# One of the seven products per tile of gate and up done in plain float32

## The chip, the cores and the metric

The kernel runs on one core of one Trainium2 chip. The core has four engines that compute, each with its own stream of instructions: TensorE (PE in the profile; its weight loads are PEld), VectorE (DVE), ScalarE (ACT) and GpSimd (POOL). A fifth, SyncE (SP), issues the DMAs here. The metric is the device time of one execution in microseconds (us); lower is better.

## The reference

Two layers of a decoder trunk on 512 tokens of width 1024. Each layer has two feed-forward blocks ("macaron half-steps"), a token mixer of three head groups, and a gated input embedding. The change lies in the feed-forward blocks, of which there are four in all. Their hidden width is 2816:

```python
def swiglu(x, w_in, w_out):
    gate, up = jnp.split(x @ w_in, 2, axis=-1)
    return (jax.nn.silu(gate) * up) @ w_out

  x += 1/2 * post(SwiGLU_a(pre(x)))
  ...
  x += 1/2 * post(SwiGLU_b(pre(x)))
```

`pre` and `post` are RMS norms with a gain. All inputs are float32.

## The kernel before

**Products in parts.** Most products on TensorE take operands of type `fp32r`. Each operand is split into a high and a low part: ScalarE copies the source into the high part, which rounds it (`split`, L140), and VectorE, or POOL where the caller says so, subtracts that from the source to get the low part (L141). `mm3` (L162 to L164) then makes three matmuls for each block of 128 rows: high by high, high by low, low by high. The product of the two low parts is left out.

**Tiles of the hidden features.** `ffn` goes over 22 tiles (m = 0 to 21) of 128 gate features and the same 128 up features. The weights of a tile come in two DMAs (L311), as g1, g2, u1, u2: gate and up by halves of the 1024 inputs, each 128x512. The 512 tokens are halved too, L and H. The four blocks of the product are made by Winograd's form of Strassen's method, with seven products of half size in place of eight. POOL makes four sums of the tile's weights (L353 to L356, `ws`). The seven left operands are g1, g2, u2 as they are (products 1, 2, 4) and the sums s1 to s4 (products 5, 6, 7, 3). Each is split into parts (`wsplit`), so a tile has seven splits, called w1 to w7 after their products. Their buffers come from a pool of six. A product has four blocks of 128 inputs, three matmuls each with 256 tokens: 12 matmuls, 84 for a tile.

**The right operands.** They are made once per block by `turn`, from the normed and transposed input, for tokens by quarters. Halves of the inputs by halves of the tokens serve products 1, 2, 3 and 5 (`xh`, `xl`); three sums, t2, t3 and t4, serve products 6, 7 and 4, and are split into the three tiles `tx`. t4 is written over a part of `xr` (L237) and then split, ScalarE's copy and POOL's subtraction, in the loop at the end of `turn`.

**The combination.** VectorE adds the products out of PSUM: L362 (product 6), L367 (product 2), L365 (products 7 and 5), L369 (product 3), L370, L373 (product 4); ScalarE applies silu (L371); VectorE multiplies gate by up into `h` (L376). Product 3 writes the other half of the bank that L362 reads, and starts only after L362. The four PSUM tiles are `p12` (products 1 and 2), `p63`, `p75` and `p4`.

**The order.** The code is written tile by tile, but a scheduler with a timeline of its own sets the order of each engine's instructions when the program is built. In the middle of the loop it works one tile ahead: VectorE splits the weights of tile m + 1 while it combines tile m. On TensorE the order is 6, 7, 5, the beginning of 4, 3, the rest of 4, and then 1 and 2 of the next tile. The raw weights `wr` go through slots that are also used by the `tx` tiles (six of tag `q`): three are left for the weights, so a slot serves the tile three later.

After the 22 tiles, `ffn_out` makes the second product from `h` with the output weights, again with splits on ScalarE and VectorE, sums on POOL, and matmuls at L466. Its first splits and sums are mixed into the last tiles of the loop.

**Plain float32 elsewhere.** The mixer has some matmuls on float32 operands that are not split, among them L970 in `rwkv_back`: two calls of 256 columns for each half of the tokens.

Of the kernel before, what the change touches and what calls it, by code (L numbers as in the profile page):

```python
# [10 lines left out]
F32R = mybir.dt.float32r  # L11
I32 = mybir.dt.int32
AF = mybir.ActivationFunctionType
ALU = mybir.AluOpType
# [7 lines left out]
EPS = 1e-6  # L22
# [51 lines left out]
class Trunk:  # L74
# [50 lines left out]
    def lanes(self, main=MAINL, aux=AUXL, chain=""):  # L125
        """The PSUM tags that the two kinds of tiles go through in turn."""
        self.main, self.aux = cycle(main), cycle(aux)
        self.chain = chain
# [19 lines left out]
    def wblock(self, ap, name, slot=False, raw=None, eng=None):  # L148
        """A block of weights as two halves, each with its high and low parts."""
        c = ap.shape[1]  # L150
        if raw is None:
            raw = self.wraw.tile([128, c], F32, tag="raw", name=name + "_r")
        self.nc.sync.dma_start(out=raw, in_=ap)
        if slot:
            w = self.slot("h", [2, c], name, F32R)
            self.split(w[:, 0], w[:, 1], raw, eng)
            return [(w[:, 0, i * c // 2:(i + 1) * c // 2], w[:, 1, i * c // 2:(i + 1) * c // 2]) for i in range(2)]
        return [self.wsplit(raw[:, i * c // 2:(i + 1) * c // 2], name, eng) for i in range(2)]
# [17 lines left out]
    def rms(self, ss, scale=1.0):  # L176
        """scale / sqrt(mean + EPS) from two halves of the mean square, each over scale squared."""
        g_ = self.nc.gpsimd
        v, r = self.small("v"), self.small("r")
        g_.tensor_scalar(v, ss[0], ss[1], EPS / (scale * scale), op0=ALU.add, op1=ALU.add)  # L180
        g_.tensor_tensor(r, v, self.mhalf, ALU.pow)
        return r

    def ssq(self, src, name, scale=1.0, dve=False):
        """A half's part of the mean square, over scale squared."""
        junk = self.tmp.tile([128, 512], F32, tag="sg", name="junk")
        s = self.small(name)
        if dve:
            self.nc.vector.tensor_tensor_reduce(junk, src, src, 1.0 / (D * scale * scale), 0.0, ALU.mult, ALU.add, s)
            return s  # L190
        self.nc.scalar.activation(junk, src, AF.Square, scale=D ** -0.5 / scale, accum_out=s)
        return s
# [12 lines left out]
    def turn(self, t, xn, ffn):  # L205
        nc = self.nc
        v_, a_, g_ = nc.vector, nc.scalar, nc.gpsimd
        ps = []
        for j in range(2):
            p = self.aux_tile("xtp").rearrange("p (a b) -> p a b", a=4)  # L210
            for i in range(4):
                k = 4 * j + i
                nc.tensor.transpose(p[:, i], xn[:, k * 128:(k + 1) * 128], self.ident)  # L213
            ps.append(p)
        kss = [slice(0, 4), slice(4, 8)]
        ts = slice(t * 128, (t + 1) * 128)
        if ffn and t == 0:
            self.xr = self.slot("h", [2, 8, 128], "xr")
        if ffn and t == 2:
            self.tx = [self.slot("q", [2, 4, 256], "tx", F32R) for _ in range(3)]  # L220
        if not ffn or t < 2:
            for p, ks in zip(ps, kss):
                self.split(self.xh[:, ks, ts], self.xl[:, ks, ts], p)
                if ffn:
                    a_.activation(self.xr[:, t, ks], p, AF.Copy)
            return
        EB, E1, E3, E4 = None, g_, g_, g_
        # the sums of Winograd's form of the product by blocks
        u = t - 2
        xr = self.xr  # L230
        t2, t3 = (self.tmp.tile([128, 4, 128], F32, tag="tb0", name="tx", bufs=4) for _ in range(2))
        t1, t4 = (xr[:, u, ks] for ks in kss)
        a_.activation(t3, ps[0], AF.Copy)
        v_.tensor_tensor(t1, ps[0], t1, ALU.subtract)
        v_.tensor_tensor(t2, ps[1], t1, ALU.subtract)
        v_.tensor_tensor(t3, ps[1], t3, ALU.subtract)
        g_.tensor_tensor(t4, t4, t2, ALU.subtract)  # L237
        self.split(self.xh[:, kss[1], ts], self.xl[:, kss[1], ts], ps[1], EB)
        us = slice(u * 128, u * 128 + 128)
        self.split(self.xh[:, kss[0], ts], self.xl[:, kss[0], ts], t1, E1)  # L240
        for q, x, e in zip(self.tx, (t2, t3, t4), (None, E3, E4)):
            self.split(q[:, 0, :, us], q[:, 1, :, us], x, e)
# [14 lines left out]
    def out_proj(self, nb, part, blocks, gain, scale, after, tail):  # L257
        """Token-major product of the feature-major parts with weight blocks, post norm, residual."""
# [60 lines left out]
    def ffn(self, l, w, after):  # L319
        """The first product goes by Winograd's form of Strassen's seven products: gate and up features by halves of  # L320
        the inputs, halves of the inputs by halves of the tokens."""
        nc, tc = self.nc, self.tc
        v_, a_, g_ = nc.vector, nc.scalar, nc.gpsimd
# [6 lines left out]
        right = {1: plain(k1, L), 2: plain(k2, L), 3: plain(k2, H), 4: tx[2], 5: plain(k1, H), 6: tx[0], 7: tx[1]}  # L330
        hs = []

# [16 lines left out]
        def unit(m, r, pa, a):  # L349
# [9 lines left out]
            # an even tile has the tokens' second half first  # L359
# [12 lines left out]
            product(4, u2, pd[:, L])  # L372
# [24 lines left out]
    def ffn_out(self, hs, blocks, gain, scale, after):  # L397
        """Token-major product of the features with the output weights, by halves of the model's columns. Some of the
        pairs of feature tiles go by Winograd's form of Strassen's products: halves of the tokens by the tiles of the
        pair by halves of the columns."""  # L400
# [5 lines left out]
        # where the halves of a pair's tiles lie, so that the three that products take as they are lie together  # L406
# [149 lines left out]
    def fm_proj(self, ap, name, halves=False):  # L556
        """Feature-major projection of one 128-column tile."""
        w = self.wblock(ap, name)
        ps = self.mm_tile(name)
        for sl in ((slice(0, 256), slice(256, 512)) if halves else (slice(0, 512),)):  # L560
            for k in range(8):
                self.mm3(ps[:, sl], [q[:, k % 4 * 128:k % 4 * 128 + 128] for q in w[k // 4]],
                         [q[:, k, sl] for q in (self.xh, self.xl)], k == 0, k == 7)
        return ps

    def tm_proj(self, aps, cols, name, eng=None):
        """Token-major projection; aps hold the rows in k order. Tokens share a bank where they fit."""
# [83 lines left out]
    def weave(self, l):  # L651
        """The chains of the three mixers, their pieces in the order of the plan; a chain that writes its output over
        the projections' inputs lets the last projection go first."""
# [47 lines left out]
    def rwkv_prep(self, l):  # L701
        """RWKV-7 heads in chunks of 64 tokens. A unit is a chunk c of a pair p of heads; its removal-key and key
        rows are stacked on the partitions, the removal-key rows on half (c + p) % 2."""
# [22 lines left out]
        for p in range(2):  # L726
# [9 lines left out]
            # decay and in-context rate  # L736
# [9 lines left out]
            # normalised removal key  # L746
# [18 lines left out]
            # k (1 + (a - 1) k_a)  # L765
# [6 lines left out]
            # bonus  # L772
# [8 lines left out]
    def rwkv_scores(self):  # L781
# [5 lines left out]
        # token-major keys and values; the values are centered over each head, which centers the outputs  # L787
# [18 lines left out]
        # masked scores of [keys, queries] and the part of the solve's right side that values give  # L806
# [33 lines left out]
        # the removal queries token-major  # L840
# [11 lines left out]
    def rwkv_solve(self, q):  # L852
        """The merged inverse for four chunks, applied to the values' part and to the removal queries, which it
        replaces. Yields between tiles."""
# [6 lines left out]
        # a half of a bank's partitions belongs to one half of the rows  # L861
# [17 lines left out]
    def rwkv_scan(self):  # L879
        """The recurrence over the chunks."""  # L880
# [15 lines left out]
        for c in range(8):  # L896
            st, ns = sts[c % 2], sts[(c + 1) % 2]
            tk = slice(c * 64, (c + 1) * 64)
            if c < 7:
                # the diagonal blocks of the pairs' states  # L900
                pS = self.aux_tile("pst")[:, 0:128].rearrange("p (a t) -> p a t", a=2)
# [44 lines left out]
    def rwkv_norm(self, yt, eng):  # L946
        """Group norm of the centered heads."""
# [13 lines left out]
    def rwkv_back(self, yt, j):  # L961
        """The way back to feature-major, bonus and output gate."""
# [15 lines left out]
    def invert_blocks(self, sm, z, w):  # L978
        """The blocks of 16 of z = (I - M^T)^-1, for the strictly triangular blocks of 64 whose M^T are in sm."""
# [22 lines left out]
    def invert_merge(self, q, sm, z, w):  # L1002
        """Blocks of 16 merged into blocks of 64, for eight units."""
# [31 lines left out]
    def mlstm_proj(self, l):  # L1035
# [4 lines left out]
        # queries and keys through the causal convolution  # L1040
# [27 lines left out]
        # values, gates  # L1068
# [19 lines left out]
        # running maximum  # L1088
# [38 lines left out]
    def mlstm(self, l):  # L1127
        """The chunks of mLSTM, 128 tokens each."""
# [161 lines left out]
    def attention(self, l):  # L1290
# [10 lines left out]
        # high and low parts: the queries' on the halves of the partitions, the keys' on both  # L1301
# [26 lines left out]
        def softmax(t, g):  # L1328
            # the keys of this tile and the last one, the even tile's first
# [188 lines left out]
```

## Time and profile before

| | |
|---|---|
| runs | 2371.49, 2371.92, 2373.13 us; median 2371.92 |
| the profiled execution | span 2369.3 us from the first instruction to the last, 2.6 us below the median of the runs |
| mean granted TensorE clock | 0.977 of full speed |
| TensorE busy | 2142.1 us (90%), 16592 matmul records |
| VectorE busy | 2019.5 us (85%) |
| ScalarE busy | 1159.0 us (49%) |
| POOL busy | 1215.5 us (51%) |
| HBM | 199.23 MB read, 87 GB/s over the span |

The page is read from its shares down to single instructions. A row of a group has the line, the engine, the operation, what is written and read (out<-in, by the program's names without numbers), the shape, the count, and behind the first bar the busy time in us and the mean ns of one; behind the second stands the idle time of the engine just before such instructions, and what ended it. A row of a timeline has the start in us, the length in us, and the instruction; an entry in square brackets is the idle time before it and its releaser. The length of a matmul includes its way through the array, so matmuls overlap, and the time that each one costs is the distance between starts. The same holds, by some 0.08 us, for VectorE. A row of windows has the stretch, its length, the busy time and the count of PE, PEld, DVE, ACT and POOL, the granted clock, the share of the DMA engines and GB/s. A row for one line has min/median/max in ns, the first and last start, and the form.

The four blocks' loops end, by the `h` of their last tile, near 301, 1003, 1471 and 2171 us.

### The profile page before, as it was taken

How to read it: one execution, taken by the hardware profiler on the slowest of the kernel's cores; microseconds unless marked ns; L12 is line 12 of the kernel's file. 1: busy time of each engine (PE TensorE's matmuls, PEld its weight loads, DVE VectorE, ACT ScalarE, POOL GpSimd, SP SyncE). 2: the span in 40 equal slices, each digit the busy share in tenths (PEclk: the TensorE clock that was granted, in tenths of full speed). 3: DMA queues.
4: the chain of work that ended last, by engine and by line, in shares of the span. 5: the costliest groups of instructions: out<-in, count | busy, mean ns of one | idle time of the engine just before them, and what ended most of it. 6: DMA issues, size and time to landing. Idle time of an engine off the chain costs nothing. (4 is left out here: it accounts for less than half of the span.)

```text
span 2369.3 us, 42540 instructions
## 1 busy us (share of the span) xinstructions
PE 2142.1 (90%) x16592; PEld 1975.2 (83%) x16592; DVE 2019.5 (85%) x2990; ACT 1159.0 (49%) x2262; POOL 1215.5 (51%) x1088
## 2 busy tenths in 40 slices
PE   5899988999998899988989989889999989989898
PEld 5888887988778888887878888888887789889787
DVE  8999999645768999998689999986557699999984
ACT  4444544546545444545554445444474454445443
POOL 5665476132236665566365655751332466555751
PEclk8999999999999999999999999999999999999999
DMA  3222222422031222123411221233220312222232
GB/s 151 90 89 90 71 90 90 147 81 55 20 142 54 86 93 90 63 90 116 134 71 72 92 105 55 84 120 122 68 63 7 143 72 90 90 90 75 78 107 80
DMA packets 67513, 208.78 MB, mean 88 GB/s; under 512 B 15728, under 2 KB 16752, under 8 KB 67312
## 3 DMA queue, kind: packets, MB, share of 16 engines
q1 hardware_dynamic: 67312, 206.07, 25.2%
q8 instruction: 130, 2.13, 0.4%
q14 instruction: 71, 0.58, 0.1%
HBM read 199.23 MB, written 6.82 MB: 87 GB/s over the span
## 5 line engine op out<-in xcount | busy, mean ns | idle before, releaser
L162 PE MATMUL p<-xh,w 128*128 128x256 f32 x1408 | 407.8, 291 | 79.8 <-DVE gate L362 77.5
L164 PE MATMUL p<-xh,w 128*128 128x256 f32 x1408 | 401.6, 286 | 13.6 <-DVE w L141 13.6
L163 PE MATMUL p<-xl,w 128*128 128x256 f32 x1408 | 400.8, 285 | 0.1
L141 DVE TENSOR_TENSOR w<-wr,w 128x512 fp32r<-128x512 f32 x249 | 374.8, 1528 | 10.0 <-ACT w L140 9.8
L140 ACT ACTIVATE w<-ws 128x512 fp32r<-128x512 f32 x352 | 210.6, 623 | 305.0 <-POOL ws L354 178.2
L162 PEld LDWEIGHTS p<-xh,w 128*128 128x128 f32 x1408 | 269.9, 192 | 95.5 <-DVE gate L362 89.7
L141 DVE TENSOR_TENSOR w<-ws,w 128x512 fp32r<-128x512 f32 x352 | 327.7, 935 | 3.2 <-ACT w L140 3.1
L162 PE MATMUL p<-tx,w 128*128 128x256 f32 x1056 | 299.9, 285 | 19.1 <-ACT tx L140 14.7
L164 PE MATMUL p<-tx,w 128*128 128x256 f32 x1056 | 298.9, 284 | 5.3 <-DVE w L141 5.2
L163 PE MATMUL p<-tx,w 128*128 128x256 f32 x1056 | 299.2, 284 | 4.7 <-DVE tx L141 4.7
L164 PEld LDWEIGHTS p<-xh,w 128*128 128x128 f32 x1408 | 270.9, 192 | 14.8 <-DVE w L141 14.8
L353 POOL TENSOR_TENSOR ws<-wr 128x512 f32<-128x512 f32 x88 | 119.0, 1352 | 316.2 <-issue 299.5
L163 PEld LDWEIGHTS p<-xl,w 128*128 128x128 f32 x1408 | 270.8, 192 | 0.7 <-DVE xl L141 0.7
L162 PEld LDWEIGHTS p<-tx,w 128*128 128x128 f32 x1056 | 204.7, 194 | 21.2 <-ACT tx L140 15.3
L164 PEld LDWEIGHTS p<-tx,w 128*128 128x128 f32 x1056 | 203.3, 193 | 7.4 <-DVE w L141 7.1
L163 PEld LDWEIGHTS p<-tx,w 128*128 128x128 f32 x1056 | 203.7, 193 | 5.6 <-DVE tx L141 5.6
L466 PE MATMUL y<-wo,hq 128*128 128x256 f32 x1536 | 189.4, 282 | 3.2 <-DVE up L373 2.7
L140 ACT ACTIVATE w<-wr 128x512 fp32r<-128x512 f32 x264 | 163.3, 625 | 57.7 <-PE p L164 41.9
L466 PEld LDWEIGHTS y<-wo,hq 128*128 128x128 f32 x1536 | 184.5, 189 | 4.8 <-DVE up L373 3.5
L355 POOL TENSOR_TENSOR ws<-wr 128x512 f32<-128x512 f32 x88 | 145.9, 1658 | 46.7 <-DVE w L141 45.0
L354 POOL TENSOR_TENSOR ws<-ws,wr 128x512 f32<-128x512 f32 x88 | 147.4, 1675 | 0.6
L356 POOL TENSOR_TENSOR ws<-wr,ws 128x512 f32<-128x512 f32 x88 | 142.4, 1618 | 5.6
(436 smaller groups left out, 5613.4 us busy)
## 6 DMA issues: line engine op xcount, KB each, us to landing
wr<-in_w_ffn_in SPq DMA_DIRECT2D x176, 512.0 KB, 4.1
ws_r<-in_w_ffn_out SPq DMA_DIRECT2D x56, 512.0 KB, 3.2
wo_r<-in_w_ffn_out SPq DMA_DIRECT2D x32, 512.0 KB, 3.3
pkrv_r<-in_w_rw SPq DMA_DIRECT2D x16, 512.0 KB, 3.5
wpg_r<-in_w_ple_gate SPq DMA_DIRECT2D x16, 512.0 KB, 3.4
xd<-x SPq DMA_DIRECT2D x8, 512.0 KB, 2.9
x<-xd SPq DMA_DIRECT2D x8, 512.0 KB, 3.5
pq_r<-in_w_q SPq DMA_DIRECT2D x8, 512.0 KB, 3.5
```

What stands on the lines that cost most here:

```text
L140: self.nc.scalar.activation(hi, src, AF.Copy)
L141: (eng or self.nc.vector).tensor_tensor(lo, src, hi.bitcast(F32), ALU.subtract)
L162: mm(out, a[0], b[0], start=first, stop=False)
L163: mm(out, a[0], b[1], start=False, stop=False)
L164: mm(out, a[1], b[0], start=False, stop=last)
L353: g_.tensor_tensor(s1, u1, u2, ALU.add)
L354: g_.tensor_tensor(s2, s1, g1, ALU.subtract)
L355: g_.tensor_tensor(s3, g1, u1, ALU.subtract)
L356: g_.tensor_tensor(s4, g2, s2, ALU.subtract)
L466: nc.tensor.matmul(banks[n][:, u], a[:, x, u * 128:u * 128 + 128], b[y], start=n not in seen, stop=last and i == 2, skip_group_check=True)
```

## The change

Product 4, u2 by t4, is done with plain float32 operands. t4 is kept as it is in a float32 tile of its own, `t4`, which takes the slot that the third `tx` tile had; its split (one copy on ScalarE, one subtraction on POOL, for each of two quarters of the tokens) is gone. u2 is read by TensorE from the raw weights; its split w4 (one copy on ScalarE, one subtraction on VectorE) is gone. In place of 12 matmuls on parts there are four calls on float32. The diff, without the lines that only take away comments (lines of code move by up to four):

```diff
-            self.tx = [self.slot("q", [2, 4, 256], "tx", F32R) for _ in range(3)]
+            self.tx = [self.slot("q", [2, 4, 256], "tx", F32R) for _ in range(2)]
+            self.t4 = self.slot("q", [4, 256], "t4")
...
-        g_.tensor_tensor(t4, t4, t2, ALU.subtract)
+        g_.tensor_tensor(self.t4[:, :, u * 128:u * 128 + 128], t4, t2, ALU.subtract)
...
-        for q, x, e in zip(self.tx, (t2, t3, t4), (None, E3, E4)):
+        for q, x, e in zip(self.tx, (t2, t3), (None, E3)):
...
-        right = {1: plain(k1, L), 2: plain(k2, L), 3: plain(k2, H), 4: tx[2], 5: plain(k1, H), 6: tx[0], 7: tx[1]}
+        right = {1: plain(k1, L), 2: plain(k2, L), 3: plain(k2, H), 5: plain(k1, H), 6: tx[0], 7: tx[1]}
...
+        t4 = self.t4
...
-            product(4, u2, pd[:, L])
+            for k in range(4):
+                nc.tensor.matmul(pd[:, L], u2[:, k * 128:(k + 1) * 128], t4[:, k], start=k == 0, stop=k == 3)
```

The scheduler orders the engines anew. VectorE in the middle of a block's loop before the change, from the split w5 of one tile to the split w6 of the next (the numbers in names are those of tiles; gate_1203 belongs to one tile of features, wr_1328 and wr_1458 to the next two):

```order
L141 TENSOR_TENSOR w5_1405<-ws_1364,w5_1405 128x512
L373 TENSOR_TENSOR up_1244<-p4_1243,up_1244 128x256
L141 TENSOR_TENSOR w3_1422<-ws_1365,w3_1422 128x512
L376 TENSOR_TENSOR h_939<-gate_1203,up_1244 128x512
L141 TENSOR_TENSOR w4_1440<-wr_1328,w4_1440 128x512
L141 TENSOR_TENSOR w1_1463<-wr_1458,w1_1463 128x512
L362 TENSOR_TENSOR gate_1332<-p63_1370,gate_1332 128x256
L141 TENSOR_TENSOR w2_1478<-wr_1458,w2_1478 128x512
L367 TENSOR_TENSOR gate_1332<-p12_1331,gate_1332 128x256
L141 TENSOR_TENSOR w6_1504<-ws_1494,w6_1504 128x512
```

And the same stretch of the changed kernel, where L362, L367, L369, L370, L373 and L376 have become L364, L369, L371, L372, L377 and L380:

```order
L141 TENSOR_TENSOR w5_1313<-ws_1272,w5_1313 128x512
L371 TENSOR_TENSOR gate_1122<-p63_1160,up_1163 128x256
L372 TENSOR_TENSOR up_1163<-p75_1161,up_1163 128x256
L141 TENSOR_TENSOR w3_1330<-ws_1273,w3_1330 128x512
L377 TENSOR_TENSOR up_1163<-p4_1162,up_1163 128x256
L380 TENSOR_TENSOR h_880<-gate_1122,up_1163 128x512
L141 TENSOR_TENSOR w1_1360<-wr_1355,w1_1360 128x512
L141 TENSOR_TENSOR w2_1375<-wr_1355,w2_1375 128x512
L364 TENSOR_TENSOR gate_1240<-p63_1278,gate_1240 128x256
L141 TENSOR_TENSOR w6_1401<-ws_1391,w6_1401 128x512
```

The split w4 is gone; w2 now stands ahead of the instruction that product 3 waits for, and the two additions for product 3 (L371, L372) stand behind w5 and no longer ahead of it.

TensorE before, at the end of product 3 and over the rest of product 4 (`tx`) to product 1 of the next tile:

```order
L164 MATMUL p63_1112<-xh_87,w3_1164 128x256
L162 MATMUL p4_1114<-tx_217,w4_1182 128x256
L163 MATMUL p4_1114<-tx_217,w4_1182 128x256
L164 MATMUL p4_1114<-tx_217,w4_1182 128x256
L162 MATMUL p4_1114<-tx_217,w4_1182 128x256
L163 MATMUL p4_1114<-tx_217,w4_1182 128x256
L164 MATMUL p4_1114<-tx_217,w4_1182 128x256
L162 MATMUL p4_1114<-tx_217,w4_1182 128x256
L163 MATMUL p4_1114<-tx_217,w4_1182 128x256
L164 MATMUL p4_1114<-tx_217,w4_1182 128x256
L162 MATMUL p12_1202<-xh_87,w1_1204 128x256
```

And in the changed kernel:

```order
L163 MATMUL p63_1160<-xl_88,w3_1212 128x256
L164 MATMUL p63_1160<-xh_87,w3_1212 128x256
L376 MATMUL p4_1162<-t4_217,wr_1118 128x256 x2
L162 MATMUL p12_1239<-xh_87,w1_1241 128x256
L163 MATMUL p12_1239<-xl_88,w1_1241 128x256
```

Three matmuls of product 4 stood ahead of product 3 and nine behind it; now two calls stand ahead and two behind, and they read the raw weights `wr`. On POOL the order of the four sums of a tile is now s1, s2, s3, s4; it was s1, s3, s2, s4.

## The prediction

> **What bounds the kernel now.** I read the page first, then the stretches by windows, then one tile's timeline on each engine. The page's engine line, and the tile loop of the first and the last of the four feed-forward blocks by windows (window, then busy time of each engine with its count):
>
> ```profile
> PE 2142.1 (90%) x16592; PEld 1975.2 (83%) x16592; DVE 2019.5 (85%) x2990; ACT 1159.0 (49%) x2262; POOL 1215.5 (51%) x1088
> ```
> ```profile
> 99.00:246.00 147.00, 132.35 (x1094) 129.65 (x1094) 146.55 (x184) 64.96 (x118) 86.70 (x57) 1.00 0.26 94
> ```
> ```profile
> 1969.00:2115.00 146.00, 133.59 (x1107) 131.14 (x1106) 145.55 (x182) 66.08 (x119) 85.70 (x57) 1.00 0.26 95
> ```
>
> Over the whole span TensorE looks the busier, but in the loop that the change touches VectorE has no idle time (146.55 of 147) and TensorE has 10% of it. What TensorE waits for is in the groups of instructions (busy, mean ns | idle before, releaser):
>
> ```profile
> L162 PE MATMUL p<-xh,w 128*128 128x256 f32 x1408 | 407.8, 291 | 79.8 <-DVE gate L362 77.5
> L141 DVE TENSOR_TENSOR w<-wr,w 128x512 fp32r<-128x512 f32 x249 | 374.8, 1528 | 10.0 <-ACT w L140 9.8
> ```
>
> 77.5 us in four blocks of 22 tiles, 0.88 us a tile, is the wait of product 3 for VectorE's L362. One tile of that loop, VectorE's timeline (start, length, what), then POOL's:
>
> ```profile
> 209.51 0.42 DVE L373 TENSOR_TENSOR up<-p,up 128x256 f32<-128x256 f32 x1
> 209.84 1.75 DVE L141 TENSOR_TENSOR w<-ws,w 128x512 fp32r<-128x512 f32 x1
> 211.52 0.68 DVE L376 TENSOR_TENSOR h<-gate,up 128x512 f32<-128x512 f32 x1
> 212.12 3.47 DVE L141 TENSOR_TENSOR w<-wr,w 128x512 fp32r<-128x512 f32 x2
> 215.51 0.41 DVE L362 TENSOR_TENSOR gate<-p,gate 128x256 f32<-128x256 f32 x1
> 215.85 1.43 DVE L141 TENSOR_TENSOR w<-wr,w 128x512 fp32r<-128x512 f32 x1
> 217.20 0.41 DVE L367 TENSOR_TENSOR gate<-p,gate 128x256 f32<-128x256 f32 x1
> 217.53 0.68 DVE L141 TENSOR_TENSOR w<-ws,w 128x512 fp32r<-128x512 f32 x1
> 218.13 0.68 DVE L365 TENSOR_TENSOR up<-p,gate 128x512 f32<-128x512 f32 x1
> 218.73 0.68 DVE L141 TENSOR_TENSOR w<-ws,w 128x512 fp32r<-128x512 f32 x1
> 219.33 0.41 DVE L369 TENSOR_TENSOR gate<-p,up 128x256 f32<-128x256 f32 x1
> 219.78 0.42 DVE L370 TENSOR_TENSOR up<-p,up 128x256 f32<-128x256 f32 x1
> 220.12 0.68 DVE L141 TENSOR_TENSOR w<-ws,w 128x512 fp32r<-128x512 f32 x1
> 220.72 0.42 DVE L373 TENSOR_TENSOR up<-p,up 128x256 f32<-128x256 f32 x1
> ```
> ```profile
> 209.73 1.32 POOL L353 TENSOR_TENSOR ws<-wr 128x512 f32<-128x512 f32 x1 [4.21 <-issue]
> 211.67 1.67 POOL L355 TENSOR_TENSOR ws<-wr 128x512 f32<-128x512 f32 x1 [0.63 <-DVE w L141]
> 213.31 1.73 POOL L354 TENSOR_TENSOR ws<-ws,wr 128x512 f32<-128x512 f32 x1
> 215.12 1.61 POOL L356 TENSOR_TENSOR ws<-wr,ws 128x512 f32<-128x512 f32 x1
> ```
>
> From L373 to the next L373 a tile takes 11.21 us, with VectorE always at work. Seven of its instructions are weight splits (L141). Three of them come every 0.60 us (217.53 to 218.13); the four that meet a POOL instruction take 1.68, twice 1.70 (212.12 to 215.51) and 1.35. Add start and length: POOL's L353 ends at 211.05, the split beside it at 211.59; L354 at 215.04, the split at 215.59; L356 at 216.73, the split at 217.28. Each ends 0.54 to 0.55 after POOL, as if it began only then, while L362, with an operand in PSUM, took its usual 0.41 while L356 ran. So about 4.0 of the 11.21 us are blocks by POOL, one for each of its four sums a tile: 1.08 + 2.19 + 0.75 over the 0.60 that a split takes alone. VectorE's own work is 7.19.
>
> **The change, part by part.** *TensorE.* Rows of its timeline: matmuls of the `tx` kind (products 4, 6, 7), 16 steps between these two, and of the `xh` kind (1, 2, 3, 5), 22 steps between the next two:
>
> ```profile
> 154.85 0.28 PE L162 MATMUL p<-tx,w 128*128 128x256 f32 x1
> 156.66 0.28 PE L163 MATMUL p<-tx,w 128*128 128x256 f32 x1
> ```
> ```profile
> 151.29 0.29 PE L162 MATMUL p<-xh,w 128*128 128x256 f32 x1
> 153.91 0.28 PE L163 MATMUL p<-xl,w 128*128 128x256 f32 x1
> ```
>
> That is 0.113 and 0.119 us a matmul. A tile's 36 and 48 are 4.07 + 5.71 = 9.78 us. Product 4's twelve (1.36 us) go. For four plain float32 matmuls of 256 columns the trace has an example in the mixer, L970, where two calls in the code (p = 0, 1) are four records:
>
> ```profile
> 687.09 1.03 PE L970 MATMUL pgf<-xg,arena 128*128 128x256 f32 x4
> 687.98 0.44 PE L1141 MATMUL pym<-ident,mg 128*128 128x128 f32 x2
> ```
> ```profile
> L970 PEld LDWEIGHTS pgf<-xg,arena x16: 190/190/192, 672.5 to 1855.0; 128*128 128x128 f32 x16
> L970 PE MATMUL pgf<-xg,arena x16: 379/379/382, 672.6 to 1855.2; 128*128 128x256 f32 x16
> ```
>
> So each call is two passes, and a pass comes every (1.03 - 0.379) / 3 = 0.217 us, with its 0.19 us weight load hidden. Four calls are eight passes, 1.74 us: TensorE gains work, 0.38 us a tile. The next instruction starts 0.89 us after the first pass, and four passes at 0.217 are 0.87, so I add nothing for going in and out. New TensorE tile: 2.71 + 5.71 + 1.74 = **10.16 us** without waits.
>
> *VectorE.* The split of u2 goes: 0.60 of own work, or 1.70 if its block by POOL goes with it. The order shows what stands there: w3, L377, h, w1, w2, and the L364 that was L362. The sums on POOL remain, so the blocks can fall on w3, h, w1 and w2, where `h` was free until now. All four kept: 7.19 - 0.60 + 4.02 = 10.61 us. One fewer, 9.6. TensorE's 10.16 lies between; POOL's first sum now runs beside L371 and L372, which read PSUM, so I expect part of one block to go, and small mutual waits. I take **10.4 us**, a gain of 0.81 a tile, with 10.16 (1.05) and 10.61 (0.60) as ends. All 22 tiles of a block count at this price: the first and the last ones are uneven, but VectorE is as full there (54.17 of 56 us):
>
> ```profile
> 246.00:302.00 56.00, 50.27 (x403) 48.89 (x402) 54.17 (x70) 27.76 (x48) 28.15 (x21) 0.97 0.20 67
> ```
>
> 88 x 0.81 = 71 us.
>
> *ScalarE* loses a copy of some 0.6 us a tile, and was idle for more than half of it (64.96 of 147): nothing.
>
> *Start of each block.* The splits of t4 go, two copies and two POOL subtractions a block:
>
> ```profile
> L140 ACT ACTIVATE tx<-xr x8: 612/623/632, 33.8 to 1922.3; 128x512 fp32r<-128x512 f32 x8
> L141 POOL TENSOR_TENSOR tx<-xr,tx x8: 1289/1722/1751, 34.5 to 1924.7; 128x512 fp32r<-128x512 f32 x8
> ```
>
> They stand ahead of the first tiles' sums on POOL. At most 2 x (1.72 + 0.62) = 4.7 us a block, at least nothing; I take 1.2, so 5 us in all.
>
> *Loads.* The raw weights of a tile are now free after the last pass of product 4 on TensorE, not after VectorE's split. The slot serves the tile three later. A load lands in 4.1 us from issue:
>
> ```profile
> wr<-in_w_ffn_in SPq DMA_DIRECT2D x176, 512.0 KB, 4.1
> ```
>
> From the end of product 4 of one tile to the sums that need the slot's next content lie products 1, 2, 6, 7, 5, half of 4 and 3, some 9 us. Two loads one behind the other fit, and nothing is charged; were that cover gone, POOL's sums would start late by the difference. Behind those issues on SP stand only the next tiles' loads.
>
> **Sum.** 71 + 5 = 76 us from the profiled execution's 2369.3 gives 2293.3; the median of the runs is 2.6 above that span, so **2296**.
>
> **The rivals.**
>
> *VectorE stays the bound.* If POOL's four sums still block four instructions in full, only the 0.60 of own work goes and a tile takes 10.6 to 10.75 us: 88 x 0.46 to 0.60, with 0 to 5 us at the starts, is 2314 to 2331. For it: every split that meets POOL ends 0.54 us after POOL's end, and the new order has four candidates. Against it: L371 and L372 now lie beside the first sum.
>
> The Trainium skill, "SBUF — State Buffer", section "Who interferes with whom", states this as a rule: a VectorE instruction with two SBUF inputs and a GpSimd instruction that reads SBUF exclude each other, and the later one blocks until the first is done. By that rule the time charged to w4 is mostly not its own and passes to a neighbour; the end times above agree with the rule.
>
> *Product 3 still waits.* Two splits, w1 and w2, now stand ahead of L364. From the end of one product 3, VectorE has L371, L372, w3, L377, h, w1, w2, L364: 0.45 + 0.34 + 1.68 + 0.33 + 3 x 1.70 + 0.34 = 8.2 us; TensorE has half of 4, then 1, 2, 6, 7, 5, and half of 4: 0.87 + 2.86 + 2.71 + 1.43 + 0.87 = 8.7. The slack is 0.5 us. If VectorE starts later by more than that, the wait returns and a tile takes 10.8 to 11.0: 2338 to 2356.
>
> *Slower: the weight loads show.* If passes in plain float32 waited for their loads, eight would take 8 x (0.217 + 0.19) = 3.26 us, TensorE's tile 11.68, and 88 x 0.47 = 41 us would be added: 2413. It turns against the change from 2.79 us for the eight passes (11.21 - 8.42), 0.35 each. L970's records speak against it.
>
> *Nothing comes of it*, because a later load or another wait takes the place: within 0.2%, which is about what a measurement of this kernel can tell from no change.
>
> *More than the sum.* TensorE alone sets the pace at 10.16 and the uneven tiles gain up to a whole 1.70: 2264 to 2277.
>
> **How the numbers follow.** The forecast, 10.25 to 10.55 us a tile with 0 to 10 us at the starts, is 2278 to 2314: chance 0.50. VectorE still the bound 0.22; product 3 waits 0.10; more than the sum 0.10; nothing 0.03; slower 0.05. The range 2264 to 2331 holds the first two and most of "more". Faster 0.50 + 0.22 + 0.10 + 0.10 = 0.92, within 0.2% 0.03, slower 0.05.
>
> **What would show it.** Right: the tile near 10.4 us; the wait for L364 at a few us in place of 77.5; VectorE's w<-wr group at 161 instead of 249; the plain matmuls as 704 records at 0.217 us. With POOL's blocks complete, VectorE stays without idle time and the tile is at 10.6. A wait for L364 near 0.5 us a tile speaks for product 3. Passes at 0.35 us or more would make the prediction wrong in sign, and so would POOL's sums waiting for loads.

## The result, and the profile after

The changed kernel takes 2287.37 us (median of 4 runs, 2284.53 to 2289.04), the kernel before 2371.7 us (median of 4 runs beside them). The ratio is 0.9644, with a 95% interval of 0.9631 to 0.9658. The profiled execution has a span of 2285.2 us, 84.1 less than before.

The page after the change, its engine line (busy, share of the span, instructions) and three of its groups of instructions:

```profile
PE 2144.9 (94%) x16240; PEld 1971.8 (86%) x16240; DVE 1902.7 (83%) x2902; ACT 1121.0 (49%) x2166; POOL 1210.1 (53%) x1080
...
L162 PE MATMUL p<-xh,w 128*128 128x256 f32 x1408 | 424.1, 302 | 12.9 <-DVE gate L364 9.7
...
L141 DVE TENSOR_TENSOR w<-wr,w 128x512 fp32r<-128x512 f32 x161 | 261.6, 1659 | 9.4 <-ACT w L140 9.4
...
L376 PE MATMUL p<-t,wr 128*128 128x256 f32 x704 | 178.2, 378 | 0.0
```

TensorE is as busy as before (2144.9 against 2142.1 us): nothing came from less work there. What went is its wait for VectorE ahead of product 3, 9.7 us for L364 where L362 had 77.5. VectorE lost 88 splits and 117 us of busy time. The plain matmuls are 704 records, and TensorE waits for nothing ahead of them.

The changed kernel by windows, a stretch of 100 us in the middle of the first block's loop (busy time of PE, PEld, DVE, ACT and POOL, then granted clock, DMA share, GB/s):

```profile
120.00:220.00 100.00, 99.54 (x783) 97.14 (x782) 98.61 (x126) 46.25 (x79) 68.01 (x44) 1.00 0.29 106
```

In the same loop TensorE was busy for 132.35 of 147 us before. Now TensorE and VectorE are both at 99%, so one row doesn't tell which of them sets the pace.

VectorE's timeline of the changed kernel, over one tile of that loop and the split w5 just ahead of it:

```profile
202.25 0.67 DVE L141 TENSOR_TENSOR w<-ws,w 128x512 fp32r<-128x512 f32 x1
202.85 0.41 DVE L371 TENSOR_TENSOR gate<-p,up 128x256 f32<-128x256 f32 x1
203.30 0.42 DVE L372 TENSOR_TENSOR up<-p,up 128x256 f32<-128x256 f32 x1
203.64 1.28 DVE L141 TENSOR_TENSOR w<-ws,w 128x512 fp32r<-128x512 f32 x1
204.85 0.41 DVE L377 TENSOR_TENSOR up<-p,up 128x256 f32<-128x256 f32 x1
205.36 1.26 DVE L380 TENSOR_TENSOR h<-gate,up 128x512 f32<-128x512 f32 x1
206.54 3.48 DVE L141 TENSOR_TENSOR w<-wr,w 128x512 fp32r<-128x512 f32 x2
209.95 0.41 DVE L364 TENSOR_TENSOR gate<-p,gate 128x256 f32<-128x256 f32 x1
...
213.01 0.41 DVE L371 TENSOR_TENSOR gate<-p,up 128x256 f32<-128x256 f32 x1
```

POOL's timeline of the changed kernel in that tile:

```profile
203.06 1.31 POOL L355 TENSOR_TENSOR ws<-wr 128x512 f32<-128x512 f32 x1 [3.75 <-issue]
204.45 1.62 POOL L356 TENSOR_TENSOR ws<-ws,wr 128x512 f32<-128x512 f32 x1
206.03 1.74 POOL L357 TENSOR_TENSOR ws<-wr 128x512 f32<-128x512 f32 x1
207.74 1.74 POOL L358 TENSOR_TENSOR ws<-wr,ws 128x512 f32<-128x512 f32 x1
```

A tile takes 10.16 us here (202.85 to 213.01), against 11.21 before. Distances between starts give the blocks by POOL, over the 0.60 us that such an instruction takes alone: w3 (203.64 to 204.85) 0.61, `h` (205.36 to 206.54) 0.58, w1 and w2 together (206.54 to 209.95) 2.21. That is 3.40 us, where it was 4.02. Each blocked instruction still ends 0.54 to 0.55 us after the end of a POOL instruction: 204.92 after 204.37, 206.62 after 206.07, 210.02 after 209.48. The new piece is at the top: L371 and L372, whose operands come from PSUM, lie beside most of POOL's first sum and take their usual 0.41. From L377 to `h`, which reads its result, are 0.51 us, 0.17 more than an instruction of this length takes elsewhere. VectorE's tile by these terms is 7.19 - 0.60 + 3.40 + 0.17 = 10.16, exactly what the forecast gave TensorE.

Why w3 is blocked for less can be read from the split w5 ahead of it. VectorE's timeline of the kernel before has it here:

```profile
208.91 0.68 DVE L141 TENSOR_TENSOR w<-ws,w 128x512 fp32r<-128x512 f32 x1
```

In both kernels POOL's first sum starts 0.13 to 0.14 us after w5 ends (209.73 after 209.59 before, 203.06 after 202.92 now; the traces of e1, e2 and e11 show the same 0.13). So what stands right behind w5 in VectorE's order meets that sum. Before it was one addition and then w3, which started 0.93 us after w5's start and lost 1.08. Now it is two additions, w3 starts after 1.39 us and loses 0.61: it starts 0.46 us later and loses 0.47 less.

TensorE's timeline of the changed kernel, around the first half of product 4:

```profile
201.91 0.28 PE L164 MATMUL p<-xh,w 128*128 128x256 f32 x1
202.03 1.02 PE L376 MATMUL p<-t,wr 128*128 128x256 f32 x4
202.70 0.47 PE L162 MATMUL p<-xh,w 128*128 128x256 f32 x1
203.01 0.28 PE L163 MATMUL p<-xl,w 128*128 128x256 f32 x1
```

Two calls are four passes. A pass comes every (1.02 - 0.378) / 3 = 0.214 us. The next matmul's record starts early (202.70) and is longer than its kind (0.47), but the one behind it starts 0.98 us after the first pass: 4 x 0.214 and one usual step of 0.12. Going into plain float32 and out of it shows no cost here.

To see where the 84 us came from, each block is cut in four at instructions that all kernels have: from the last matmul of the output product to the next block's first `tx` matmul ("between": norms, mixer, `turn`), to the `h` of the fifth tile ("start"), to that of the 18th ("middle", 13 tiles), to the last matmul of the output product ("end"). Sums over the four blocks in us, worked out from the ends of these instructions in the traces (the start, for the first `tx` matmul); the "rest" lies after the last one:

| | between | start (20 tiles) | middle (52) | end (16, with the output product) | rest |
|---|---|---|---|---|---|
| before | 750.9 | 214.3 | 586.5 | 751.7 | 66.0 |
| after | 744.7 | 197.7 | 532.5 | 744.1 | 66.2 |
| difference | -6.2 | -16.6 | -54.0 | -7.6 | +0.2 |

The middle gives 1.04 us a tile, the end 0.48. The borders are soft: `h` itself moved in VectorE's order and is blocked now, so 2 or 3 us of the sums can belong to the stage beside.

### The profile page after: what moved, and what is told of

Same layout as the page of the kernel before. It is cut to its first block, busy times and chain, and to the rows that moved or that the text cites. A ratio compares the mean times of both kernels' runs of the same rounds, so it can differ in the third digit from the quotient of the medians.

```text
span 2285.2 us, 41718 instructions
## 1 busy us (share of the span) xinstructions
PE 2144.9 (94%) x16240; PEld 1971.8 (86%) x16240; DVE 1902.7 (83%) x2902; ACT 1121.0 (49%) x2166; POOL 1210.1 (53%) x1080
## 3 DMA queue, kind: packets, MB, share of 16 engines
q1 hardware_dynamic: 67312, 206.07, 26.1%
## 5 line engine op out<-in xcount | busy, mean ns | idle before, releaser
L162 PE MATMUL p<-xh,w 128*128 128x256 f32 x1408 | 424.1, 302 | 12.9 <-DVE gate L364 9.7
L164 PE MATMUL p<-xh,w 128*128 128x256 f32 x1408 | 398.6, 284 | 7.5 <-DVE w L141 7.5
L140 ACT ACTIVATE w<-ws 128x512 fp32r<-128x512 f32 x352 | 219.0, 630 | 307.4 <-PE p L164 246.3
L141 DVE TENSOR_TENSOR w<-ws,w 128x512 fp32r<-128x512 f32 x352 | 300.5, 858 | 7.6 <-ACT w L140 7.5
L141 DVE TENSOR_TENSOR w<-wr,w 128x512 fp32r<-128x512 f32 x161 | 261.6, 1659 | 9.4 <-ACT w L140 9.4
L162 PE MATMUL p<-tx,w 128*128 128x256 f32 x704 | 200.6, 286 | 11.5 <-ACT tx L140 11.5
L164 PE MATMUL p<-tx,w 128*128 128x256 f32 x704 | 198.0, 282 | 1.8 <-DVE w L141 1.8
L163 PE MATMUL p<-tx,w 128*128 128x256 f32 x704 | 198.8, 283 | 0.7 <-DVE tx L141 0.5
L376 PE MATMUL p<-t,wr 128*128 128x256 f32 x704 | 178.2, 378 | 0.0
L358 POOL TENSOR_TENSOR ws<-wr,ws 128x512 f32<-128x512 f32 x88 | 153.0, 1739 | 0.9
L470 PE MATMUL y<-wt,xh 128*128 128x256 f32 x768 | 122.9, 297 | 24.9 <-DVE xh L141 15.1
L162 PEld LDWEIGHTS p<-tx,w 128*128 128x128 f32 x704 | 135.0, 192 | 12.5 <-ACT tx L140 12.2
L452 POOL TENSOR_TENSOR wt_r<-ws_r 128x512 f32<-128x512 f32 x56 | 96.6, 1724 | 91.6 <-DMA ws_r<-in_w_ffn_out 78.0
L356 POOL TENSOR_TENSOR ws<-ws,wr 128x512 f32<-128x512 f32 x88 | 140.6, 1598 | 5.7
```

The costliest lines, as they stand in the source:

```text
L140: self.nc.scalar.activation(hi, src, AF.Copy)
L141: (eng or self.nc.vector).tensor_tensor(lo, src, hi.bitcast(F32), ALU.subtract)
L162: mm(out, a[0], b[0], start=first, stop=False)
L163: mm(out, a[0], b[1], start=False, stop=False)
L164: mm(out, a[1], b[0], start=False, stop=last)
L356: g_.tensor_tensor(s2, s1, g1, ALU.subtract)
```

## The experiments

Two questions were open. Does TensorE or VectorE set the 10.16 us, and is the gain of 1.05 us a tile the split's own 0.60 or something of its block? Diffs are against the changed kernel unless another is named. Each ratio is against the kernel before, run beside it. The last column is the usual distance from `h` to `h` in the middle; one tile in each block, in which POOL also makes four sums for the output product, takes 0.7 to 0.9 us longer before and after the change.

| run | median us | ratio, 95% interval | tile in the middle, us |
|---|---|---|---|
| changed kernel | 2287.37 | 0.9644, 0.9631 to 0.9658 | 10.17 |
| e1_split_kept | 2334.08 | 0.9854, 0.9825 to 0.9882 | 10.78 |
| e2_hi_only | 2294.05 | 0.9685, 0.9657 to 0.9713 | 10.18 |
| e3_two_plain | 2292.13 | 0.9677, 0.9649 to 0.9705 | 10.55 |
| e4_twice | 2406.70 | 1.016, 1.0131 to 1.019 | 11.93 |
| e5_hi_s4_vector | 2256.76 | 0.9526, 0.9498 to 0.9554 | 9.68 |
| e6_t4_split_kept | 2295.58 | 0.969, 0.9662 to 0.9718 | 10.2 |
| e7_edges | 2280.38 | 0.9626, 0.9597 to 0.9655 | 10.2 |
| e8_out_plain | 2276.64 | 0.961, 0.9582 to 0.9638 | 10.2 |
| e9_s4_vector | 2273.23 | 0.9592, 0.9573 to 0.9611 | 9.8, then 10.2 |
| e10_s4_out | 2263.55 | 0.955, 0.9536 to 0.9564 | 9.8, then 10.2 |
| e11_before_sums_order | 2386.92 | 1.0072, 1.0052 to 1.0092 | 11.44 |
| e12_s4_edges_out | 2267.06 | 0.9567, 0.9551 to 0.9583 | 9.8, then 10.2 |

**e1: plain product 4, and the split kept though nothing reads it.**

```diff
+            self.wsplit(u2, "w4")
             for k in range(4):
                 nc.tensor.matmul(pd[:, L], u2[:, k * 128:(k + 1) * 128], t4[:, k], start=k == 0, stop=k == 3)
```

> The changed kernel, but u2 is still split into parts (ScalarE copy, VectorE subtraction) that nothing reads; product 4 stays plain. Theory A (the gain is VectorE's missing instruction): a tile in the middle of the loop goes back to about 11.2 us, and the time to 2355 to 2372 us, the start of the blocks alone staying shorter. Theory B (the gain comes from fewer matmul instructions or weight loads on TensorE): the middle tile stays near 10.2 us and the time near 2287.

Measured: 2334.08 us, a tile of 10.78. VectorE's timeline of this kernel:

```profile
201.83 0.41 DVE L371 TENSOR_TENSOR gate<-p,up 128x256 f32<-128x256 f32 x1
...
202.61 1.29 DVE L141 TENSOR_TENSOR w<-ws,w 128x512 fp32r<-128x512 f32 x1
203.82 0.41 DVE L378 TENSOR_TENSOR up<-p,up 128x256 f32<-128x256 f32 x1
204.34 1.27 DVE L381 TENSOR_TENSOR h<-gate,up 128x512 f32<-128x512 f32 x1
205.54 3.48 DVE L141 TENSOR_TENSOR w<-wr,w 128x512 fp32r<-128x512 f32 x2
208.94 0.41 DVE L364 TENSOR_TENSOR gate<-p,gate 128x256 f32<-128x256 f32 x1
209.27 0.68 DVE L141 TENSOR_TENSOR w<-wr,w 128x512 fp32r<-128x512 f32 x1
...
212.61 0.41 DVE L371 TENSOR_TENSOR gate<-p,up 128x256 f32<-128x256 f32 x1
```

VectorE does the seven splits of before, but with L371 and L372 behind w5, as in the changed kernel; the blocked pair is now w4 and w1, and w2 is free at 0.68. Neither number of the theories came out. Of the 1.05 us a tile, 0.44 (11.22 to 10.78) are there with the split kept, and 0.60 (10.78 to 10.18, below) go with it. The blocks are 3.4 us with the split and without: taking an instruction away took only its own work, and the rest came from the new order, above all from w3's later start behind w5.

**e2: the kernel before, with the split of u2 gone and product 4 reading the high part of s4 in its place** in four calls on fp32r, so that u2 by t4 is left out of the result:

```diff
-            product(3, s4, pc[:, H])
+            q3 = self.wsplit(s4, "w3")
+            product(3, q3, pc[:, H])
...
-            product(4, u2, pd[:, L])
+            for k in range(4):
+                nc.tensor.matmul(pd[:, L], q3[0][:, k * 128:(k + 1) * 128], right[4][0][:, k], start=k == 0, stop=k == 3)
```

> The kernel before, without the split of u2, and with only four matmuls for product 4, the high parts of s4 by those of t4 (so the product is not the reference's, and t4 is still split). VectorE's and POOL's orders are those of the changed kernel; TensorE's tile is 2.71 + 5.71 + 0.45 = 8.9 us in place of 10.16. Theory A (TensorE sets the pace of the changed kernel's middle tiles): the middle tile falls below 10.17, to VectorE's own limit of 9.6 to 10.05 us, and the time to 2265 to 2285. Theory B (VectorE sets the pace, and 10.17 beside TensorE's 10.16 is chance): it stays within 0.05 of 10.17, or at 10.6 with all of POOL's blocks, and the time is no lower than 2285.

Measured: 2294.05 us, a tile of 10.18. This kernel by windows:

```profile
120.00:220.00 100.00, 89.60 (x739) 87.55 (x739) 98.61 (x129) 44.57 (x78) 65.41 (x43) 1.00 0.31 106
```

TensorE is idle for a tenth of the time, VectorE is as full as in the changed kernel, and the tile is the same. So theory B has the number: VectorE's own limit, without w4, is 10.18 us, and TensorE's 10.16 happens to lie beside it. The whole is 6.7 us above the changed kernel; t4 is still split here. Its middle is 6.3 us shorter and its start 10.9 longer, but most of that is a matter of the border: the `h` of the fifth tile stands behind one more blocked split (1.7 us) in each block. Start and middle together take 734.8 us, not 730.2.

**e3: product 7 plain as well**, t3 kept beside t4, s3 not split:

```diff
-            self.tx = [self.slot("q", [2, 4, 256], "tx", F32R) for _ in range(2)]
-            self.t4 = self.slot("q", [4, 256], "t4")
+            self.tx = [self.slot("q", [2, 4, 256], "tx", F32R)]
+            t34 = self.slot("q", [2, 4, 256], "t4")
+            self.t3, self.t4 = t34[:, 0], t34[:, 1]
...
-            product(7, s3, pb[:, P])
+            for k in range(4):
+                nc.tensor.matmul(pb[:, P], s3[:, k * 128:(k + 1) * 128], t3[:, k], start=k == 0, stop=k == 3)
```

> The changed kernel with product 7 plain too (s3 by t3, kept as they are; splits of both gone). Each tile of TensorE gets 0.38 us longer (10.54), VectorE loses one more split. Theory A (TensorE sets the pace in the middle tiles): 10.5 to 10.6 us a middle tile, the ends of the blocks a little shorter, time 2290 to 2315. Theory B (VectorE sets it): a middle tile falls by 0.6 or more to 9.6 us and the time to 2230 to 2250.

Measured: 2292.13 us, a tile of 10.55. This kernel by windows:

```profile
120.00:220.00 100.00, 100.00 (x725) 96.12 (x724) 74.91 (x116) 38.95 (x68) 55.53 (x42) 1.00 0.31 106
```

VectorE has a quarter of the time to spare, TensorE none, and the tile is TensorE's 10.16 + 0.38 = 10.54, as theory A had it. The second exchange of a split for plain passes is past the point where it pays in the middle: 16.4 us more there (548.9 against 532.5), while the starts, at 182.8, are still quicker by 14.9.

**e4: the four calls of product 4 made twice**, the second time into the unused half of its PSUM tile:

```diff
-            for k in range(4):
-                nc.tensor.matmul(pd[:, L], u2[:, k * 128:(k + 1) * 128], t4[:, k], start=k == 0, stop=k == 3)
+            for e in range(2):
+                for k in range(4):
+                    nc.tensor.matmul(pd[:, (L, H)[e]], u2[:, k * 128:(k + 1) * 128], t4[:, k], start=k == 0, stop=k == 3)
```

> The changed kernel with the plain product 4 done twice (a second time into the other half of the bank, where nothing reads it). TensorE gets 8 x 0.217 = 1.74 us a tile more. Theory A: a middle tile goes to 11.9 us and the time to 2420 to 2440. If VectorE had slack over TensorE (theory B), it would rise by less than 1.2 us a tile, to below 2395. It also measures what a plain pass costs in this place: 0.217 us as in the mixer, or 0.23 and more if going in and out of float32 costs something.

Measured: 2406.70 us, a tile of 11.93 with TensorE always busy. Eight more passes cost 11.93 - 10.17 = 1.76 us, 0.22 each, in line with the 0.214 of the timeline. Weight loads do not show. The total is below what was expected from 88 tiles, 119 us and not 153, since the first and last tiles pay less.

**e5: e2 with one of POOL's four sums done by VectorE** (against e2):

```diff
-            g_.tensor_tensor(s4, g2, s2, ALU.subtract)
+            v_.tensor_tensor(s4, g2, s2, ALU.subtract)
```

> The kernel of e2_hi_only (product 4 from the high parts alone, of s4 and t4, so not the reference's), with the sum s4 made by VectorE and no longer by POOL. In e2 VectorE had no idle time at 10.18 us a tile. Theory A (a POOL sum holds one VectorE instruction up for some 1.1 us and then lets it run at its own 0.6): VectorE gets 0.60 of work and loses one block of 1.10, so a middle tile falls to 9.6 to 9.8 us and the time to 2250 to 2270. Theory B (the longer times of VectorE's splits are not caused by POOL): the tile rises by 0.6 to 10.8 and the time to 2340.

Measured: 2256.76 us, a tile of 9.68. VectorE's timeline of this kernel:

```profile
201.59 1.28 DVE L141 TENSOR_TENSOR w<-ws,w 128x512 fp32r<-128x512 f32 x1
202.80 0.41 DVE L375 TENSOR_TENSOR up<-p,up 128x256 f32<-128x256 f32 x1
203.14 1.46 DVE L141 TENSOR_TENSOR w<-wr,w 128x512 fp32r<-128x512 f32 x1
204.52 1.77 DVE L378 TENSOR_TENSOR h<-gate,up 128x512 f32<-128x512 f32 x1
206.22 0.68 DVE L356 TENSOR_TENSOR ws<-wr,ws 128x512 f32<-128x512 f32 x1
206.82 0.68 DVE L141 TENSOR_TENSOR w<-wr,w 128x512 fp32r<-128x512 f32 x1
207.42 0.41 DVE L362 TENSOR_TENSOR gate<-p,gate 128x256 f32<-128x256 f32 x1
```

VectorE got more work, 0.60 us a tile, and became faster by 0.50: the sum (L356) comes with the step of 0.60. The blocks, by distances between starts, are w3 0.61, w1 0.78 and `h` 1.10, in all 2.49 us for three sums on POOL, where e2 has 3.41 for four. The 0.17 us that `h` waited behind product 4's addition (L375) is gone too, since w1 now stands between them: 0.60 - 0.92 - 0.17 = -0.49. VectorE's order is not quite e2's, so the 0.92 is the worth of one sum fewer in the order that came with it. The Trainium skill, "SBUF — State Buffer", section "Who interferes with whom", calls what the two engines contend for an exclusive lock; the 0.92 us of blocks that went with one sum agree with that.

**e6: the changed kernel with the split of t4 done as before**, its result unread:

```diff
-            self.t4 = self.slot("q", [4, 256], "t4")
+            t4 = self.slot("q", [2, 4, 256], "t4")
+            self.t4, self.t4p = t4[:, 0], t4[:, 1]
...
+        a_.activation(self.t4p[:, :, us], self.t4[:, :, us], AF.Copy)
+        g_.tensor_tensor(self.t4p[:, :, us], self.t4[:, :, us], self.t4p[:, :, us], ALU.subtract)
```

> The changed kernel, but t4 is still split at the start of each block, by a ScalarE copy and a POOL subtraction, into a place that nothing reads. The prediction put 5 us (0 to 19) on the absence of this split. Theory A: the starts, from a block's first product 6 to its fifth tile, take 1 to 2 us longer each, the rest is unchanged, time 2289 to 2295. Theory B (the starts are shorter because of the splits of u2 alone): no difference within 2 us.

Measured: 2295.58 us, 8.2 above the changed kernel (9.7 by the spans, 11 by the ratios). The start stage is 207.4 us and not 197.7; "between" is 4.8 longer, and middle and end are 4.5 shorter. So the absence of t4's split is worth 8 to 11 us, where the prediction took 5 between bounds of 0 and 19, and a start gains some 2.4 us, more than the 1 to 2 expected.

**e7: product 7 plain too, in the first four and the last four tiles alone:**

```diff
...
-            product(7, s3, pb[:, P])
+            if m < 4 or m > 17:
+                for k in range(4):
+                    nc.tensor.matmul(pb[:, P], s3[:, k * 128:(k + 1) * 128], t3[:, k], start=k == 0, stop=k == 3)
+            else:
+                product(7, s3, pb[:, P])
```

> The changed kernel with product 7 plain as well, but only in tiles 0 to 3 and 18 to 21 of each block; in the middle tiles as in the changed kernel. If the first and last tiles are held by VectorE (theory A), the starts gain what e3 gained there (about 3 us each) and the ends about 1 us, while the middle stays at 10.17 us: 2266 to 2278. If the gain of e3's starts came from the missing split of t3, which is made here (theory B): 2280 to 2290.

Measured: 2280.38 us; the span is 4.4 below the changed kernel's. The ends give 5.0 (739.1 for 744.1), start and "between" together nothing. That is theory B's time, and at the limit of what these runs resolve.

**e8: products 1 and 2 of the output product plain**, so that its hidden features and weights have fewer splits:

```diff
-            self.split(x[:, 0, 0:3], x[:, 1, 0:3], r[:, 1:])
+            self.split(x[:, 0, 2], x[:, 1, 2], r[:, 3])
...
-            b0, b1 = self.wsplit(r[:, 0, L], "wb"), self.wsplit(r[:, 1], "wb")
+            b3 = self.wsplit(r[:, 1, H], "wb")
...
-            return {1: b0, 2: cut(b1, L), 3: cut(b1, H), 4: tt(3), 5: tt(0), 6: tt(2), 7: tt(1)}
+            return {1: r[:, 0, L], 2: r[:, 1, L], 3: b3, 4: tt(3), 5: tt(0), 6: tt(2), 7: tt(1)}
...
+                nc.tensor.matmul(banks[n][:, u], a[:, u * 128:u * 128 + 128], b, start=n not in seen,
+                                 stop=last, skip_group_check=True)
...
```

> The changed kernel, with products 1 and 2 of each pair in the output product plain as well (their operands, quarters of h and of the weights, are there unsplit). From the last tiles of the loop to the end of the output product VectorE is the fuller engine (125 of some 139 us after the last h). It loses 128x768 elements of splits a pair of 12 to 14 pairs a block, 0.6 to 2 us each with POOL's blocks; TensorE gets 2 x (2 x 2 x 0.217 - 6 x 0.119) = 0.3 us a pair more. Theory A (VectorE is the bound there): 8 to 20 us less a block, time 2205 to 2255. Theory B (POOL's sums or the loads are, or the raw weights are held too long by TensorE): 2275 to 2295.

Measured: 2276.64 us, 10.7 below the changed kernel and in theory B's range. The end stage is 28.6 us shorter (715.5), but "between" is 13.7 longer and the rest 4.9: 18.6 of the 28.6 come back right behind the output product. Which instruction there gives them back was not traced.

**e9: e5's edit in the changed kernel** (the line of s4 as in e5).

> The changed kernel with the sum s4 on VectorE in place of POOL, product 4 plain. e2 took the load off TensorE alone and left a middle tile at 10.18 us, e5 took it off both and gave 9.68. This takes it off VectorE alone. Theory A (in the changed kernel TensorE, 10.16, and VectorE, 10.18, both stand at their limits): the middle tile stays at 10.16 to 10.2; the last tiles and the output product, where VectorE is fuller, gain what e5 gained there, some 3 us a block: 2268 to 2278. Theory B (VectorE alone sets the pace): 9.7 us a tile and 2235 to 2255.

Measured: 2273.23 us, 14.1 below the changed kernel. VectorE's timeline of this kernel, from the top of one tile to that of the next:

```profile
199.95 0.42 DVE L371 TENSOR_TENSOR gate<-p,up 128x256 f32<-128x256 f32 x1 [0.87 <-PE p L164]
...
202.69 1.66 DVE L358 TENSOR_TENSOR ws<-wr,ws 128x512 f32<-128x512 f32 x1
...
210.15 0.42 DVE L371 TENSOR_TENSOR gate<-p,up 128x256 f32<-128x256 f32 x1 [0.87 <-PE p L164]
```

This is the counterpart of e2. VectorE now has 0.87 us a tile to spare here and waits for TensorE's product 3, and the tile stays at 10.20 us: TensorE's own limit is nearly the same number (10.1 to 10.3 by block and tile). Nearer the start of each block VectorE is still behind TensorE and not yet held by it: there its tiles take 9.8 us, while TensorE does only 76 or 77 matmuls of its 80 between two `h`. The 14 us come from the ends, where the stage falls to 729.4, by 14.7; the middle's 6.6 less and 7.0 more ahead of it offset each other.

**e10: e8 and e9 together.**

> e9 and e8 together: s4 on VectorE, and products 1 and 2 of the output product's pairs plain. Both act where VectorE is the fuller engine, at the end of each block. If their gains add, 10 us for e8 and that of e9: 2258 to 2268. If the end of the block is limited by another engine once VectorE has less to do: no better than the better of the two.

Measured: 2263.55 us, the quickest of the kernels that do the whole computation. The gains add: 10.7 + 14.1 = 24.8, and 23.8 is measured.

**e11: the kernel before with the sums on POOL in the order s1, s2, s4, s3**, to see whether POOL's order alone gives the 0.44 us of e1. s3 is written over g1, so it comes after all that reads g1, and last (against before):

```diff
+            s3 = g1
             g_.tensor_tensor(s3, g1, u1, ALU.subtract)
```

> The kernel before, with s3 written over g1, which makes POOL do s1, s2, s4, s3 with no wait for VectorE's split w3 in between; VectorE's order is that of before (w5, L374, w3, h, w4, w1). e1 has the same seven splits as the kernel before and takes 10.78 us a tile instead of 11.22. Theory A (the 0.44 comes from VectorE's order: two additions out of PSUM behind w5, beside POOL's first sum): no such gain here, 11.0 to 11.3 us and 2355 to 2375. Theory B (it comes from POOL's order s1, s2 first): about 10.8 us and 2320 to 2340.

Measured: 2386.92 us, a tile of 11.44. VectorE's timeline of this kernel:

```profile
201.71 0.42 DVE L374 TENSOR_TENSOR up<-p,up 128x256 f32<-128x256 f32 x1
202.05 1.76 DVE L141 TENSOR_TENSOR w<-ws,w 128x512 fp32r<-128x512 f32 x1
203.73 1.79 DVE L377 TENSOR_TENSOR h<-gate,up 128x512 f32<-128x512 f32 x1
205.45 2.38 DVE L141 TENSOR_TENSOR w<-wr,w 128x512 fp32r<-128x512 f32 x2
207.75 0.41 DVE L363 TENSOR_TENSOR gate<-p,gate 128x256 f32<-128x256 f32 x1
208.08 1.65 DVE L141 TENSOR_TENSOR w<-wr,w 128x512 fp32r<-128x512 f32 x1
209.65 0.41 DVE L368 TENSOR_TENSOR gate<-p,gate 128x256 f32<-128x256 f32 x1
```

The blocks are w3 1.08, `h` 1.12, the pair 1.10 and w2 0.97: 4.27 us, 0.25 more than before, which is the 0.2 us that the tile is longer. POOL's first sum of this kernel, from its timeline:

```profile
201.93 1.33 POOL L353 TENSOR_TENSOR ws<-wr 128x512 f32<-128x512 f32 x1 [4.20 <-issue]
```

It begins 0.12 us ahead of w3 and blocks it in full; in the changed kernel and in e1 it begins while the additions for product 3 run. So there is no gain, as theory A has it, though tile and time lie above its range (up to 11.3 and 2375): with s1 and s2 first on POOL, and VectorE's order as before, the 0.44 does not come. POOL's order here is not e1's in full: s4 stands ahead of s3, and s3 waits 1.23 us for a split on VectorE and then blocks w2.

**e12: e10 with e7's edges.**

> e10 with product 7 plain in tiles 0 to 3 and 18 to 21 (e7). e7 gave some 5 us, all of it at the blocks' ends; e8 and e9 act in the same place. If VectorE is still the fuller engine there: 2254 to 2264. If not, the longer tiles of TensorE (0.38 us in eight tiles a block, 12 us in all) show: 2265 to 2275.

Measured: 2267.06 us, 3.5 above e10, with the intervals overlapping. With VectorE relieved by e9's edit, the plain product 7 at the edges is no help any more.

## Why the prediction was right

The time fell within the forecast's own case (2278 to 2314), 8.6 us below the value. By its steps:

**The bound before.** VectorE without idle time in the loop and 77.5 us of TensorE waiting for L362: confirmed. 67.8 of those are gone, and e2, where TensorE keeps a tenth to spare, is no quicker in a tile.

**TensorE's new tile, 10.16 us.** Right, within some 0.1, by e9, where VectorE waits for it at 10.1 to 10.3. The eight passes were taken at 0.217 us from the mixer's rows; they measured 0.214 in the timeline and 0.22 in e4, with loads hidden and no cost seen for going in and out.

**VectorE's removed split, 0.60 or 1.70.** It was 0.60 (e1 against the changed kernel). The block did pass to a neighbour, as the rival had it: w2, free in e1, stands in the blocked pair of the changed kernel. (`h` is blocked in both, by the new order.) What the rival priced too high is the sum of the blocks: 3.40 and not 4.02, because of where L371 and L372 now stand. The prediction named that ("part of one block to go"), and with the 0.62 it measured and 0.17 lost between L377 and `h`, VectorE's limit is 10.61 - 0.62 + 0.17 = 10.16.

**The choice of 10.4 us.** Mis-sized: 10.17. I had added small mutual waits between two engines with nearly the same limit. They hardly arose: product 3 waits for L364 for 9.7 us in 88 tiles, 0.11 us each, and both engines are at 99%. That VectorE's new limit came out beside TensorE's is chance; nothing in the working made them equal.

**All 22 tiles at one price.** This is the step that was wrong in kind. Its errors partly cancel, so it is in part luck that the total came so near. At 0.81 the 52 middle tiles would give 42.1 us and gave 54.0; the 16 at the ends would give 13.0 and gave 7.6. In the ends VectorE and POOL also do the output product's splits and sums, and 0.48 a tile is less than the split's own 0.60; whether the new order saves any block there was not traced. That e9 gains 14.7 us in this stage speaks for POOL and VectorE holding it up.

**The starts, 5 us for t4.** Mis-sized: 8 to 11 (e6). Start and "between" together gave 22.8, where 20 x 0.81 + 5 = 21.2 was in the sum.

**Loads and ScalarE, nothing.** L376 has no idle time ahead of it (0.0), and nothing in the middle of the loop waits for a load.

**The rivals.** "VectorE stays the bound" was half true: VectorE's limit is as near as TensorE's, at 10.18 and not at 10.6. "Product 3 still waits" gave 0.11 us a tile; its 2338 to 2356 counted the 2.6 us between span and runs twice, and 10.8 to 11.0 us a tile would give 2336 to 2353. The weight loads stay hidden. "More than the sum" had TensorE's pace right, but not the uneven tiles.

## What to carry to other kernels

An instruction that showed 1.70 us because another engine blocked it was worth its own 0.60 when it was removed: the block waited for the next one. Blocks went when the blocking engine did less (a sum moved from POOL to the full VectorE made VectorE quicker) or when instructions on PSUM stood beside it. Work out each engine's limit with the others out of the way; where two come out this near to each other, relieving either alone gains nothing more in that stage. Here e2 relieves TensorE alone and e9 VectorE alone, and each time the other engine still takes 10.2 us for its tile; e5 relieves both, and the tile falls to 9.68.

## What the runs showed of the hardware

- The order of VectorE's and POOL's instructions, with the same instructions on both, was worth 0.44 us in 11.22 (e1). POOL's sums block VectorE's instructions on two SBUF operands, which end 0.54 to 0.55 us after POOL's, and not those with an operand in PSUM (0.41 us beside a sum).
- Matmuls in plain float32 between fp32r ones cost 0.214 to 0.22 us a pass and showed no cost at either change of kind; only the record of the first one behind them is longer (0.47 for 0.28), without shifting its successor.
- Not settled: why `xh` matmuls come every 0.119 us and `tx` ones every 0.113 (in the changed kernel's tile 0.118 for product 6 and 0.114 for product 7), and where e8's 18.6 us go.
